# Keeping the split feed-forward weights in DRAM between the two token halves

## The chip, the cores and the metric

The kernel runs on one core of one Trainium2 chip. The metric is device time in microseconds for one execution of the whole layer; before the change the median of three runs is 2856.76 us (2854.7 to 2862.01).

## What is computed

One layer of a hybrid encoder on 2048 tokens of width 1024, float32 in and out. The attention part (differential attention in 4 heads, stick-breaking attention in 8) comes first and is not touched. The change lies in the last two lines, the SwiGLU feed-forward part with inner width 2816:

```
u   = rms_norm(h, norm1_w)
p   = u @ w_in                      # q, k, v of both attentions
h   = h + concat(y_diff, y_sb) @ w_out
u2  = rms_norm(h, norm2_w)
h   = h + (silu(u2 @ w_gate) * (u2 @ w_up)) @ w_down
```

## The kernel before

**Precision.** TensorE gets float16 operands, but the products are to be nearly float32. Each float32 operand is split in two float16 tiles, a rounded part `hi` and the remainder `lo`, and three products (hi·hi, lo·hi, hi·lo) are summed in PSUM.

**Strassen form.** Each of the three feed-forward products is cut in 2 x 2 blocks and computed with seven block products instead of eight (`quad` for gate and up, `down` for the third). For that the weight tile must be turned into seven block operands: four sums and differences of blocks, made in place in float32, and a split of each of the seven. The result is one tile `w16` of 128 x 7 x 2 x 512 float16 per weight and group of 256 inner columns.

**Loops.** The tokens are worked in two halves of 1024, and the inner width in NFG = 11 groups (`fg`) of 256: 22 steps, the first 11 for half 0, the rest for half 1. A step runs gate (84 matmuls), up (84) and, when two steps have been gathered, the down pass for both of them (168 matmuls) between its gate and its up. So a pair of steps is one without and one with a down pass. Residual rows are kept in DRAM (`hd`) and loaded (`hs`), added to and stored again in each down pass. The tokens' operands (`X`, seven tiles) stay in SBUF for a whole half; those of half 1 are still being built (`build_x`, with DMA transposes) while the first steps of half 0 run.

**A weight's way**, in `load_ffn`, for each of gate, up and down in every step: a stage tile `fst` (float32, 1 MB, two buffers for all three weights) is loaded. In half 0 its scale is found: ScalarE squares it into `sq` (one buffer), TensorE sums or transposes that (`fsc`), VectorE takes the maximum and makes the power-of-two scale. These scales are kept for half 1. Then, in both halves, four combinations on GpSimd (L99, three in place in `fst` and one into `sx`) and, four times, a rounding to `hi` (L210, ScalarE; now and then GpSimd) and a remainder `lo` on VectorE (L215). So each weight is loaded and split twice, once in each half, with the same result. The tiles of gate and up share two buffers (`wgu`), those of down have two (`wd`).

**Order.** Every engine runs its instructions in the order in which the program's scheduler, which has its own timeline of the program, puts them. Nearly all DMAs are issued by SP, one after the other: a DMA whose wait is not over holds up all behind it.

Of the kernel before, what the change touches and what calls it, by code (L numbers as in the profile page):

```python
# [21 lines left out]
S, D, P = 2048, 1024, 128  # L22
NT, KT, NC = S // P, D // P, S // 512
FF = 2816
NFG = FF // 256
# [14 lines left out]
XO = (10, 13, 14, 15, 11, 12, 15)  # L40
WO = (10, 14, 15)
CU = 3
WE = ("AP", "AP")
LE, SE, AE = "DP", "D", "P"


# [14 lines left out]
def block(tc, a, out):  # L61
    nc = tc.nc
    PE, ACT, DVE, POOL, SP = nc.tensor, nc.scalar, nc.vector, nc.gpsimd, nc.sync
    top = ExitStack()
    with top:
# [8 lines left out]
        def note(e, ns):  # L74
            load[e] += ns * KW[e]
# [98 lines left out]
        def across(dst, pt, cols):  # L174
            k = len(cols)
            for j, c in enumerate(cols):
                PE.matmul(pt[:, P * j : P * j + P], lhsT=c.to_broadcast([P, P]), rhs=id32[:], start=True, stop=True)
            DVE.tensor_reduce(dst, pt[:, : P * k], op=ALU.max, axis=AX.X)

        def scale_begin(pieces, junk=None):  # L180
            m0 = sm.tile([P, 4], F32, tag="m0", name=nm("m0"))
            for j, pc in enumerate(pieces):
                if junk is not None:
                    ACT.activation(junk, pc, AF.Square, accum_out=m0[:, j : j + 1])
                    note("A", 0.84 * int(np.prod(pc.shape[1:])) + 200)
                else:
                    DVE.tensor_reduce(m0[:, j : j + 1], pc, op=ALU.max, axis=AX.XY if len(pc.shape) > 2 else AX.X, apply_absolute_value=True)
                    note("D", 1.05 * int(np.prod(pc.shape[1:])) + 100)
            return [m0[:, j : j + 1] for j in range(len(pieces))]

        def scale_end(top_of, rW, pW, squares, sW):
            m1 = sm.tile([P, 1], F32, tag="m1", name=nm("m1"))
            top_of(m1[:])
            if squares:
                DVE.tensor_scalar(m1[:], m1[:], 1.0e-36, None, op0=ALU.max)
                exponents(m1[:], rW, pW)
            else:
                pow2(m1[:], rW, pW)
            DVE.tensor_scalar(sW[:], rW, 2.0 ** 10, None, op0=ALU.mult)
# [51 lines left out]
        with ExitStack() as ph1:  # L251
# [533 lines left out]
            op = out_proj()  # L785
# [13 lines left out]
        with ExitStack() as ph2:  # L799
# [14 lines left out]
            def stage(fg, nme, half):  # L814
                st = fw.tile([P, 2048], F32, tag="fst", bufs=2, name=nm("fst"))
                f0 = 256 * fg
                if nme == "d":
                    d = SP.dma_start(st[:].rearrange("p (f n) -> p f n", f=2), a["w_down"][0, f0 : f0 + 256, :].rearrange("(f p) n -> p f n", p=P))
                else:
                    d = SP.dma_start(st[:].rearrange("p (k n) -> p k n", k=KT), a["w_gate" if nme == "g" else "w_up"][0, :, f0 : f0 + 256].rearrange("(k p) n -> p k n", p=P))  # L820
                if half == 0 and fg == 0:
                    after_mt(d, WO["gud".index(nme)])
                return st

# [5 lines left out]
                    pass  # L830

            def load_ffn(half, fg, names, W):
                eng = "ADP" if half == 0 and fg == 0 else WE[half]
                sc = scales.setdefault(fg, {})
                for nme in names:
                    st = stage(fg, nme, half)
                    if half == 0:
                        r, p, sW = c1(), c1(), c1()
                        sq = fw.tile([P, 2048], BF16, tag="sq", bufs=1, name=nm("sq"))
                        if nme == "d":  # L840
                            cols = scale_begin([st[:]], sq[:])
                        else:
                            ACT.activation(sq[:], st[:], AF.Square)
                            note("A", 1900)
                    yield
                    late = nme == "d" and half == 1 and fg == NFG - 1
                    w16 = fw.tile([P, 7, 2, 512], F16, tag="wd" if nme == "d" and not late else "wgu", bufs=2, name=nm("w" + nme))
                    if half == 0:
                        pt = ps2.tile([P, 512], F32, tag="b", bufs=8, name=nm("fsc"))

                        def columns(m):
                            for k in range(KT):
                                PE.matmul(pt[:, :256], lhsT=ones[:], rhs=sq[:, 256 * k : 256 * k + 256], start=k == 0, stop=k == KT - 1)
                            DVE.tensor_reduce(m, pt[:, :256], op=ALU.max, axis=AX.X)

                        scale_end((lambda m: across(m, pt, cols)) if nme == "d" else columns, r[:], p[:], True, sW)
                        sc[nme] = (r, p, sW)
                    sW = sc[nme][2]
                    tte = "DP" if half == 0 and fg == 0 else "P"
                    sx = fw.tile([P, 512], F32, tag="sx", bufs=1, name=nm("sx"))  # L860

                    def put(o, src, n):
                        split_weight(w16[:, o : o + n, 0], w16[:, o : o + n, 1], src, 512 * n, sW, eng)

                    if nme == "d":
                        sv = st[:].rearrange("p (f h n) -> p h f n", f=2, h=2)
                        b11, b21, b12, b22 = sv[:, 0, 0], sv[:, 0, 1], sv[:, 1, 0], sv[:, 1, 1]
                        put(0, sv[:, 0], 2)
                        tt(sx[:], b22, b12, ALU.subtract, 512, tte)
                        tt(b12, b12, b11, ALU.subtract, 512, tte)  # L870
                        tt(b11, b22, b12, ALU.subtract, 512, tte)
                        tt(b21, b21, b11, ALU.subtract, 512, tte)
                        put(2, sv[:, 1], 2)
                        put(4, sv[:, 0], 2)
                        put(6, sx[:].unsqueeze(1), 1)
                    else:
                        sv = st[:].rearrange("p (d k f n) -> p d k f n", d=2, k=4, f=2)
                        xv = sx[:].rearrange("p (k n) -> p k n", k=4)
                        wv = w16[:].rearrange("p o s (k n) -> p o s k n", k=4)

                        def putk(o, src, n):
                            split_weight(wv[:, o : o + n, 0], wv[:, o : o + n, 1], src, 512 * n, sW, eng)

# [203 lines left out]
            W = {}  # L1087
# [86 lines left out]
```

## Time and profile before

| | |
|---|---|
| median of three runs | 2856.76 us |
| the profiled execution | 2849.59 us |
| its span, first to last instruction | 2847.8 us |
| mean granted TensorE clock | 0.957 |
| HBM read / written | 239.32 MB / 90.96 MB |
| `fst` loads | 66 of 1024 KB |

The feed-forward part begins at about 1480 us of the span; half 0 lasts to about 2150 and half 1 from there to the end. In the rows of groups, a line such as L99 or L215 is that of a helper that several weights use, so it is read with the tile's name. Times are from the span's start.

### The profile page before, as it was taken

Reading aid. Unit: us, or ns where it says so; the run is one execution under the profiler, and the core shown is the slowest. Engines: PE = TensorE matmul, PEld = TensorE weight load, DVE = VectorE, ACT = ScalarE, POOL = GpSimd, SP = SyncE. Lnnn points to the kernel's source line nnn. Section 1 sums busy time; section 2 is a strip of 40 time slices with the busy share of each in tenths; the row PEclk is TensorE's granted clock in tenths of the full one; section 3 lists DMA queues with packets and bytes.
Section 4 is the critical chain, followed back from the end, with each engine's and each line's share of the span. In section 5 each row is a group of like instructions: output and inputs, shape, how many; then the busy total and the mean of one; then the engine's idle time right before and its main releaser. Section 6 shows DMA issues by size and latency. Waiting matters only on the chain.

```text
span 2847.8 us, 45790 instructions
## 1 busy us (share of the span) xinstructions
PE 2519.3 (88%) x17052; PEld 1409.9 (50%) x17052; DVE 2229.5 (78%) x3922; ACT 1481.5 (52%) x2666; POOL 1703.5 (60%) x1133
## 2 busy tenths in 40 slices
PE   7998898888888777788888999899998999999997
PEld 4565556555555444477763444444443444444443
DVE  6898879787989999787638776877778868678675
ACT  4665656567787888656515443534433324334231
POOL 3577767664545545455627655656666667576663
PEclk9999999999999888999989999999999999999998
DMA  7778887889999898978876434242336442442424
GB/s 235 191 160 177 169 176 168 172 166 219 215 193 197 161 182 162 204 168 226 213 255 181 144 107 163 73 149 97 125 133 238 132 163 84 151 165 74 148 74 177
DMA packets 680094, 469.07 MB, mean 165 GB/s; under 512 B 520688, under 2 KB 610800, under 8 KB 678080
## 3 DMA queue, kind: packets, MB, share of 16 engines
q1 hardware_dynamic: 678048, 464.08, 63.1%
q8 instruction: 133, 2.18, 0.3%
q0 software_dynamic: 512, 1.36, 0.2%
q10 hardware_dynamic: 1312, 0.72, 0.1%
q14 instruction: 89, 0.73, 0.1%
HBM read 239.32 MB, written 90.96 MB: 116 GB/s over the span
## 4 chain that ended last, share of the span: by engine, by line
PE 21%; DVE 16%; DMA 7%; POOL 6%; issue 5%; ACT 3%; SPq 1%; DVEq 0%; POOLq 0%; ACTq 0%
PE pd L1008 11%; DVE wu L215 3%; PE pd L911 3%; POOL fst L99 3%; PE pm L911 3%; PE pa L911 3%; DVE wd L215 2%; DVE cg L99 2%; DMA fst<-in_w_down_dram 2%; DVE cg L976 1%; PE po L757 1%; DVE z L558 1%; DMA aT<-s 1%; DMA xcd<-b 1%; DMA b<-b 1%
## 5 line engine op out<-in xcount | busy, mean ns | idle before, releaser
L99 POOL TENSOR_TENSOR s<-z,s 128x1024 f16<-128x1024 f32 (+7 forms) x288 | 474.5, 1656 | 327.8 <-ACT s L90 299.5
L321 PE MATMUL pj<-w,xt 128*128 128x384 f16 x3072 | 576.2, 336 | 25.7 <-DVE st L331 9.6
L99 POOL TENSOR_TENSOR fst<-fst 128x512 f32<-128x512 f32 x193 | 348.3, 1805 | 225.2 <-DVE wg L215 98.0
L1008 PE MATMUL pd<-wd,act 128*128 128x512 f16 x1848 | 416.2, 384 | 30.0 <-DVE hs L1017 11.2
L321 PEld LDWEIGHTS <-xt 128*128 128x128 f16 x3072 | 301.4, 100 | 238.2 <-issue 45.0
L558 DVE TENSOR_TENSOR_SCAN z<-z,sc 128x512 f32<-128x512 f32 (+3 forms) x320 | 355.6, 1113 | 74.8 <-ACT sc L556 70.6
L449 PE MATMUL sc<-kT,qT 128*128 128x512 f16 (+3 forms) x1280 | 347.2, 362 | 72.7 <-DVE z L559 26.3
L459 PE MATMUL yp<-v,aT 128*128 128x64 f16 (+1 forms) x4896 | 281.3, 207 | 77.1 <-DMA aT<-s 76.2
L459 PEld LDWEIGHTS <-aT 128*128 128x128 f16 x4896 | 244.8, 101 | 168.6 <-DMA aT<-s 105.4
L911 PEld LDWEIGHTS <-wg 128*128 128x128 f16 x1848 | 185.8, 101 | 279.3 <-issue 76.2
L1008 PEld LDWEIGHTS <-act 128*128 128x128 f16 x1848 | 181.4, 99 | 256.6 <-issue 25.0
L911 PEld LDWEIGHTS <-wu 128*128 128x128 f16 x1848 | 182.1, 99 | 231.7 <-issue 19.2
L99 POOL TENSOR_TENSOR hs<-hs,cu 128x512 f32<-128x512 f32 x138 | 190.6, 1391 | 165.4 <-DVE cu L1017 66.4
L90 ACT CAST s<-z 128x384 f16<-128x384 f32 (+7 forms) x216 | 170.4, 790 | 139.2 <-DMA aT<-s 59.0
L1017 DVE SCALAR_TENSOR_TENSOR hs<-pd,c,hs 128x512 f32<-128x512 f32 x192 | 139.0, 745 | 131.0 <-PE pd L1008 98.6
L99 POOL TENSOR_TENSOR act<-cg,act 128x512 f16<-128x512 f32 x108 | 173.2, 1609 | 103.1 <-ACT act L970 103.1
L555 ACT ACTIVATE z<-sc,c 128x512 f32<-128x512 f32 (+3 forms) x320 | 203.8, 637 | 20.4 <-PE sc L449 10.5
L559 DVE TENSOR_TENSOR z<-sc,z 128x512 f32<-128x512 f32 (+3 forms) x320 | 193.3, 606 | 7.7
L556 ACT ACTIVATE sc<-sc,c 128x512 f32<-128x512 f32 (+3 forms) x320 | 196.0, 613 | 0.0
L757 PE MATMUL po<-wo,mt 128*128 128x256 f16 x1536 | 184.2, 279 | 13.0 <-DVE xf L760 12.5
L970 ACT CAST act<-cg 128x512 f16<-128x512 f32 x132 | 80.5, 615 | 212.1 <-DVE cg L976 124.8
L911 PE MATMUL pm<-X,wg 128*128 128x512 f16 x792 | 178.6, 379 | 1.0 <-POOL wg L214 1.0
(228 smaller groups left out, 4480.8 us busy)
## 6 DMA issues: line engine op xcount, KB each, us to landing
xt<-xs SPq DMA_DIRECT2D x112, 512.0 KB, 4.2
hs<-hd SPq DMA_DIRECT2D x96, 512.0 KB, 4.3
hd<-hs SPq DMA_DIRECT2D x80, 512.0 KB, 5.1
fst<-in_w_gate_dram SPq DMA_DIRECT2D x22, 1024.0 KB, 5.1
fst<-in_w_up_dram SPq DMA_DIRECT2D x22, 1024.0 KB, 5.3
fst<-in_w_down_dram SPq DMA_DIRECT2D x22, 1024.0 KB, 4.8
X<-xcd SPq DMA_DIRECT2D x14, 1024.0 KB, 9.6
wst<-in_w_in_dram SPq DMA_DIRECT2D x24, 512.0 KB, 6.5
```

What stands on the lines that cost most here:

```text
L90: ACT.copy(dst, src)
L99: (DVE if e == "D" else POOL).tensor_tensor(dst, a_, b_, op)
L321: PE.matmul(pj[:, :384], lhsT=xv[:, xi, kt, :], rhs=G["w"][:, wi, kt, :], start=n == 0, stop=n == 23)
L449: PE.matmul(sc[:, : 128 * w].rearrange("p (t n) -> p t n", n=P), lhsT=G["q"][i // 4][:, 2 - 2 * o + m, i % 4, :], rhs=G["k"][q][:, m, 0:w, ...
L459: PE.matmul(yp[:, y0 : y0 + wd], lhsT=aT[:, a_, :], rhs=v[:, v_ : v_ + wd], start=start and j == 0 and q == 0, stop=stop and j == nb - 1 a ...
L555: ACT.activation(om[:, lo:hi], sc[:, :w], AF.Sigmoid, scale=G["nkz"][:])
L556: ACT.activation(sc[:, :w], sc[:, :w], AF.Sigmoid, scale=G["kz"][:])
L558: DVE.tensor_tensor_scan(ov, ov, sc[:, :w], om[:, hi : hi + 1], op0=ALU.mult, op1=ALU.bypass)
L559: DVE.tensor_tensor(be[:, lo:hi], sc[:, :w], om[:, lo + 1 : hi + 1], ALU.mult)
L757: PE.matmul(po[:, sl], lhsT=mt[:, kt, P * xi : P * xi + P], rhs=wos[2 * h + n][wi][:, kt, :], start=q == 0, stop=q == 23)
L911: PE.matmul(ps_[:].rearrange("p (t n) -> p t n", n=P), lhsT=wv[:, wo, wi, 128 * kt : 128 * kt + 128], rhs=X[xo][:, :, xi, kt, :], start=st ...
L1008: PE.matmul(po[:], lhsT=act[:, ao, xi, 128 * j : 128 * j + 128], rhs=W["d"][:, wo, wi, :], start=start and u == 0 and q == 0, stop=u == nu ...
```

## The change

In half 0 the finished `w16` is also written to a DRAM tensor `split` (33 tiles of 1792 KB). In half 1 no stage tile is loaded and nothing is combined or split: the tile is read back from `split`, straight into its buffer. The engines that a split may use in half 0 stay the same (`WE[0]` and now `WE` are both ScalarE and GpSimd).

```diff
+        split = dr.tile([NFG, 3, P, 7 * 2 * 512], F16, name="split")
...
             def load_ffn(half, fg, names, W):
-                eng = "ADP" if half == 0 and fg == 0 else WE[half]
+                eng = "ADP" if fg == 0 else WE
                 sc = scales.setdefault(fg, {})
                 for nme in names:
-                    st = stage(fg, nme, half)
-                    if half == 0:
-                        r, p, sW = c1(), c1(), c1()
...
+                    if half == 1:
+                        yield
+                        late = nme == "d" and fg == NFG - 1
+                        w16 = fw.tile([P, 7, 2, 512], F16, tag="wd" if nme == "d" and not late else "wgu", bufs=2, name=nm("w" + nme))
+                        SP.dma_start(w16[:].rearrange("p o s n -> p (o s n)"), split[fg, "gud".index(nme)])
+                        W[nme] = w16
+                        continue
+                    st = stage(fg, nme)
+                    r, p, sW = c1(), c1(), c1()
...
                     W[nme] = w16
+                    SP.dma_start(split[fg, "gud".index(nme)], w16[:].rearrange("p o s n -> p (o s n)"))
```

Up to the feed-forward part the order of all engines is the same as before. Behind it the scheduler lays the work anew. Three places:

SP's queue in half 0, before, from the load of one step's gate weight on (`fst` is the stage tile, `hd` and `hs` the residual rows):

```order
L820 DMA fst_23158<-in_w_gate_dram 128x8x256
L818 DMA fst_23244<-in_w_down_dram 128x2x1024
L820 DMA fst_23339<-in_w_up_dram 128x8x256
L820 DMA fst_23500<-in_w_gate_dram 128x8x256
L818 DMA fst_23716<-in_w_down_dram 128x2x1024
L1055 DMA hd<-hs_23439 128x1024
```

and the same place now:

```order
L821 DMA fst_23182<-in_w_gate_dram 128x8x256
L899 DMA split<-wu_23093 128x7168
L819 DMA fst_23269<-in_w_down_dram 128x2x1024
L899 DMA split<-wg_23234 128x7168
L821 DMA fst_23365<-in_w_up_dram 128x8x256
L899 DMA split<-wd_23337 128x7168
L821 DMA fst_23527<-in_w_gate_dram 128x8x256
L899 DMA split<-wu_23434 128x7168
L819 DMA fst_23744<-in_w_down_dram 128x2x1024
L1061 DMA hd<-hs_23466 128x1024
```

Ahead of each stage load stands the write of the tile that was split from the same stage buffer before.

TensorE in the same step, a step of half 0 without a down pass, around the sum for the up tile's maximum (`fsc` from `sq`; `pm`, `pd`, `pa` are block products), before:

```order
L911 MATMUL pm_23364<-X_19838,wu_23070 128x512
L853 LDWEIGHTS ones
L853 MATMUL fsc_23409<-sq_23344,ones 128x256
...
L911 LDWEIGHTS wg_23210
L911 MATMUL pa_23442<-X_19828,wg_23210 128x512
...
L911 MATMUL pd_23346<-X_19840,wu_23070 128x512
```

and now:

```order
L917 MATMUL pm_23390<-X_19840,wu_23093 128x512
...
L917 MATMUL pd_23372<-X_19842,wu_23093 128x512
L858 LDWEIGHTS ones
L858 MATMUL fsc_23435<-sq_23370,ones 128x256
...
L917 MATMUL pa_23469<-X_19830,wg_23234 128x512
```

Here, and in one other of the four steady steps of half 0 without a down pass, the up tile's maximum has moved behind one more product of 12 matmuls (`pd`); in the two others it keeps its place.

VectorE in half 1, in a gate that is followed by a down pass, before (`cg` are gate blocks, `cu` up blocks, `wu` the next weight):

```order
L215 SCALAR_TENSOR_TENSOR wu_27260<-fst_27196,c_22407,wu_27260 128x2x512
L99 TENSOR_TENSOR cu_27247<-cg_27057,cg_27014 128x512
L215 SCALAR_TENSOR_TENSOR wu_27260<-fst_27196,c_22407,wu_27260 128x2x512
L927 TENSOR_TENSOR cg_27291<-pm_27293,cg_27291 128x512
L215 SCALAR_TENSOR_TENSOR wu_27260<-sx_27261,c_22407,wu_27260 128x512
L99 TENSOR_TENSOR cg_27014<-cg_27014,cg_27074 128x512
L99 TENSOR_TENSOR cg_27057<-cg_27014,cg_27057 128x512
L931 TENSOR_TENSOR cg_27320<-pm_27307,cg_27291 128x512
L99 TENSOR_TENSOR cg_27043<-cg_27043,cg_27057 128x512
L215 SCALAR_TENSOR_TENSOR wu_27260<-fst_27196,c_22407,wu_27260 128x2x512
L941 TENSOR_TENSOR cg_27351<-pd_27338,cg_27320 128x512
```

and now:

```order
L99 TENSOR_TENSOR cu_27735<-cg_27575,cg_27532 128x512
L99 TENSOR_TENSOR cg_27532<-cg_27532,cg_27590 128x512
L933 TENSOR_TENSOR cg_27767<-pm_27769,cg_27767 128x512
L99 TENSOR_TENSOR cg_27575<-cg_27532,cg_27575 128x512
L99 TENSOR_TENSOR cg_27561<-cg_27561,cg_27575 128x512
L937 TENSOR_TENSOR cg_27796<-pm_27783,cg_27767 128x512
L947 TENSOR_TENSOR cg_27825<-pd_27812,cg_27796 128x512
```

The four remainders of the split (L215) are gone from ahead of the eviction of `pd` (L941 before, L947 now), for whose buffer TensorE's next product waits. In half 1 SP's queue holds two reads for down weights at the end of each down pass and, behind them, up, gate, up, gate, each waiting for TensorE's last matmul on its buffer.

More of the change, by code (lines that the diff above doesn't have):

```diff
@@ L42 @@
 CU = 3
-WE = ("AP", "AP")
+WE = "AP"
 LE, SE, AE = "DP", "D", "P"
@@ L812, in after_mt, with stage @@
                 tc.add_manual_dep(d.ins, mts[k].ins.name, mybir.DependencyInfo(mybir.DependencyClass.NoSync, mybir.DependencyReason.DATA), reason="issue order")
-            def stage(fg, nme, half):
+            def stage(fg, nme):
                 st = fw.tile([P, 2048], F32, tag="fst", bufs=2, name=nm("fst"))
@@ L820, in stage @@
                     d = SP.dma_start(st[:].rearrange("p (k n) -> p k n", k=KT), a["w_gate" if nme == "g" else "w_up"][0, :, f0 : f0 + 256].rearrange("(k p) n -> p k n", p=P))
-                if half == 0 and fg == 0:
+                if fg == 0:
                     after_mt(d, WO["gud".index(nme)])
@@ L832, in load_ffn @@
             def load_ffn(half, fg, names, W):
-                eng = "ADP" if half == 0 and fg == 0 else WE[half]
+                eng = "ADP" if fg == 0 else WE
                 sc = scales.setdefault(fg, {})
                 for nme in names:
-                    st = stage(fg, nme, half)
-                    if half == 0:
-                        r, p, sW = c1(), c1(), c1()
[L839 to L844, printed above, removed]
-                    yield
[L846 to L857, printed above, removed]
@@ new lines, in load_ffn @@
+                    sq = fw.tile([P, 2048], BF16, tag="sq", bufs=1, name=nm("sq"))
+                    if nme == "d":
+                        cols = scale_begin([st[:]], sq[:])
+                    else:
+                        ACT.activation(sq[:], st[:], AF.Square)
+                        note("A", 1900)
+                    yield
+                    w16 = fw.tile([P, 7, 2, 512], F16, tag="wd" if nme == "d" else "wgu", bufs=2, name=nm("w" + nme))
+                    pt = ps2.tile([P, 512], F32, tag="b", bufs=8, name=nm("fsc"))
@@ L858, in load_ffn, with columns @@
+                    def columns(m):
+                        for k in range(KT):
+                            PE.matmul(pt[:, :256], lhsT=ones[:], rhs=sq[:, 256 * k : 256 * k + 256], start=k == 0, stop=k == KT - 1)
+                        DVE.tensor_reduce(m, pt[:, :256], op=ALU.max, axis=AX.X)
+                    scale_end((lambda m: across(m, pt, cols)) if nme == "d" else columns, r[:], p[:], True, sW)
+                    sc[nme] = (r, p, sW)
                     sW = sc[nme][2]
-                    tte = "DP" if half == 0 and fg == 0 else "P"
+                    tte = "DP" if fg == 0 else "P"
```

## The prediction

> **What bounds the kernel now.** I read the page's busy shares first, then busy time by stretch, the order in time of TensorE, VectorE and the DMA queue inside the feed-forward part, and the landings of the transfers.
>
> ```profile
> PE 2519.3 (88%) x17052; PEld 1409.9 (50%) x17052; DVE 2229.5 (78%) x3922; ACT 1481.5 (52%) x2666; POOL 1703.5 (60%) x1133
> ...
> 1480.00:1600.00 120.00, 104.70 (x450) 46.82 (x450) 104.35 (x152) 66.19 (x79) 81.16 (x49) 0.90 0.60 174
> 1600.00:2150.00 550.00, 515.62 (x2413) 238.64 (x2412) 406.72 (x577) 225.69 (x268) 332.35 (x212) 0.98 0.38 129
> 2200.00:2800.00 600.00, 572.27 (x2589) 255.18 (x2588) 443.45 (x441) 207.23 (x269) 392.05 (x244) 0.98 0.39 131
> ```
>
> The last three rows are the start of the first token half, the rest of it, and the second half; their columns are the stretch, then busy us and count of TensorE, weight loads, VectorE, ScalarE and GpSimd, granted clock, DMA share, GB/s. TensorE bounds both halves. How far it is from its own pace is told by the order of its work:
>
> ```profile
> 1868.23 18.29 PE L1008 MATMUL pd<-wd,act 128*128 128x512 f16 x84
> 1886.36 2.54 PE L911 MATMUL pa<-X,wu 128*128 128x512 f16 x11
> ...
> 2169.39 0.81 PE L1008 MATMUL pd<-wd,act 128*128 128x512 f16 x3
> ...
> 2201.85 3.75 PE L911 MATMUL pa<-X,wu 128*128 128x512 f16 x12
> ...
> 2318.33 2.54 PE L911 MATMUL pa<-X,wu 128*128 128x512 f16 x11
> ...
> 2742.14 2.72 PE L1008 MATMUL pd<-wd,act 128*128 128x512 f16 x11
> 2749.73 4.44 PE L911 MATMUL pd<-X,wg 128*128 128x512 f16 x12 [4.87 <-DVE cg L941]
> 2754.00 32.75 PE L1008 MATMUL pd<-wd,act 128*128 128x512 f16 x151
> 2786.59 2.54 PE L911 MATMUL pa<-X,wu 128*128 128x512 f16 x11
> ...
> 2806.66 0.81 PE L1008 MATMUL pd<-wd,act 128*128 128x512 f16 x3
> ```
>
> 84 matmuls take 1886.36 - 1868.23 = 18.13 us, 215.8 ns each. From 2201.85 (step 11's up) to 2806.66 (end of step 21's up) TensorE has 31 times 84 matmuls, 562.0 us at that pace, and takes 604.8: 42.8 us are lost. Four pairs of steps (2318.33 to 2786.59) take 117.1 us each for 108.8 of matmuls. The largest single loss is the wait for a VectorE eviction (L941) before the last gate product. Why VectorE is late there:
>
> ```profile
> 2733.30 1.56 DVE L215 SCALAR_TENSOR_TENSOR wu<-fst,c,wu 128x1024 f16<-128x1024 f32 x1 [0.65 <-ACT wu L210]
> 2736.34 2.28 DVE L215 SCALAR_TENSOR_TENSOR wu<-fst,c,wu 128x1024 f16<-128x1024 f32 x1
> 2745.04 2.28 DVE L215 SCALAR_TENSOR_TENSOR wu<-fst,c,wu 128x1024 f16<-128x1024 f32 x1
> 2748.98 0.69 DVE L941 TENSOR_TENSOR cg<-pd,cg 128x512 f32<-128x512 f32 x1
> ```
>
> VectorE has no idle of note between 2733 and 2749; the splits stand ahead of the eviction in its queue.
>
> **The second half: what goes.** Per weight tile three in-place GpSimd combinations and one into sx, four ScalarE roundings and four VectorE remainders go, for 33 tiles:
>
> ```profile
> L99 POOL TENSOR_TENSOR fst<-fst 128x512 f32<-128x512 f32 x184 | 333.2, 1811 | 190.0 <-DVE wg L215 95.7 <-DVE wd L215 47.3 <-DVE wu L215 41.0
> L215 DVE SCALAR_TENSOR_TENSOR wd<-fst,c,wd 128x1024 f16<-128x1024 f32 x63 | 100.8, 1607 | 30.2 <-ACT wd L210 30.2
> L210 ACT ACTIVATE wd<-fst,c 128x1024 f16<-128x1024 f32 x63 | 70.7, 1145 | 131.8 <-POOL fst L99 60.5 <-PE pd L1008 40.5 <-DVE c L199 16.9
> ```
>
> That frees about 33 x 4 x 1.6 = 211 us of VectorE, 33 x 4 x 1.8 = 238 of GpSimd and 33 x 4 x 1.1 = 145 of ScalarE, all beside TensorE; on the path count only the 42.8 us. VectorE falls from 443 to about 232 of 600 us, so the waits for L941 should go; I leave 1 us for each of five step pairs and take **-38** (ends -28, if a third stays, and -43). What would be late next there is the weight read.
>
> Each tile read is 7 x 2 x 512 x 2 bytes x 128 = 1.835 MB for 1.049 MB before. It is issued when the buffer's last matmul has run and is wanted, in the steps without a down pass, 61 matmuls = 13.2 us later (the sequence of products). A landing:
>
> ```profile
> X<-xcd SPq DMA_DIRECT2D x14, 1024.0 KB, 9.6
> ...
> DMA to landing us min/median/max: 4.7/5.1/14.0
> ...
> 1441.00:1449.00 8.00, 5.31 (x49) 4.61 (x48) 0.48 (x1) 0.00 (x0) 0.00 (x0) 1.00 0.98 383
> 2138.00:2150.00 12.00, 12.00 (x59) 5.63 (x57) 5.13 (x14) 3.22 (x4) 1.16 (x1) 1.00 0.98 359
> ```
>
> (median for X, queued behind one another; then the f32 stage tile; then stretches in which the rings were full, 383 and 359 GB/s.) 4.7 us for the first megabyte and 0.79 MB / 383 = 2.1 give 6.8 us: **0** (upper end: 1.75 x 9.6 = 16.8 us, 3.6 late, twice a pair, +36). I take the lower, as the DMA share here is 0.39.
>
> **The first half: what comes.** 33 writes of 1.835 MB, each issued right ahead of the stage load that takes over the buffer; the write waits for the same last remainder on VectorE as that load, so the wait itself adds nothing and SP pays 0.4 us of issue. But the load's bytes stand behind the write's: 1.835 / 383 = **4.8 us** (5.1 at 359). That transfers queue so is seen once:
>
> ```profile
> 1435.45 2.71 SPq L1097 DMA_DIRECT2D X<-xcd  x3
> ...
> 1440.50 0.38 SPq L820 DMA_DIRECT2D fst<-in_w_gate_dram  x1
> ...
> 1453.08 1.91 ACT L843 ACTIVATE sq<-fst 128x2048 bf16<-128x2048 f32 x1 [20.67 <-DMA fst<-in_w_gate_dram]
> ```
>
> A 1 MB load behind three X tiles was ready 12.6 us after its issue, for 4.7 unhindered. The HBM page of the Trainium skill (HBM Reference, Specifications) has a core that streams alone at about 425 GB/s; by that the write would hold the rings 4.3 us and the costs below would fall by about a tenth. No row here has stores alone, so I keep 383.
>
> Where is a load not covered? TensorE's maximum over a tile (fsc) needs the square (sq) of the landed tile:
>
> ```profile
> 1697.33 0.37 SPq L820 DMA_DIRECT2D fst<-in_w_up_dram  x1
> 1702.38 1.91 ACT L843 ACTIVATE sq<-fst 128x2048 bf16<-128x2048 f32 x1
> 1704.78 1.04 PE L853 MATMUL fsc<-sq,ones 128*128 128x256 bf16 x8
> ...
> 1911.36 0.38 SPq L820 DMA_DIRECT2D fst<-in_w_gate_dram  x1
> 1922.42 1.04 PE L853 MATMUL fsc<-sq,ones 128*128 128x256 bf16 x8
> ...
> 1940.74 0.37 SPq L820 DMA_DIRECT2D fst<-in_w_up_dram  x1
> 1945.84 1.91 ACT L843 ACTIVATE sq<-fst 128x2048 bf16<-128x2048 f32 x1 [0.56 <-DMA fst<-in_w_up_dram]
> 1947.80 1.86 PE L853 MATMUL fsc<-sq,ones 128*128 128x256 bf16 x8 [2.74 <-ACT sq L843]
> ```
>
> In steps without a down pass the up tile has no slack: at 1704.78 it is just in time, at 1947.80 TensorE already waits. The gate tile there has 1922.42 - 1911.36 = 11.1 us from issue to use; load 5.1, write 4.8 and square 1.9 make 11.8, about 0.9 late with the issue. So the up maximum comes 4.8 + 0.9, less 0.4 of slack, = 5.3 us later where its place stays (two of the four such steps), and 5.7 - 2.6 = 3.1 where the scheduler puts it 12 matmuls (2.6 us) later (the other two). In the steps with a down pass the maximum stands some 20 us after the load: 0, covered by the down matmuls. A stall of 5 us also slows what follows: the 12 matmuls after the wait of 4.87 took 4.44 us where 12 x 215.8 ns is 2.6, some 1.8 us. Sum 2 x (5.3 + 1.8) + 2 x 3.1 = **+20** (ends 0, if the new places hide it all, and 35).
>
> The Trainium skill (TensorE: Matmul & The Clock Gate, Part 1: The HAM clock gate) says that an idle window of about 3.4 us halves the clock until as long a busy one has passed. It agrees with the 1.8 and speaks against the change: only stalls past that length would pay it, so with all four under it the 20 would be 17.
>
> At the start (1480 to 1600) six loads in a row are tight, in two chains of three, one per stage buffer, among build_x's transposes:
>
> ```profile
> 1572.38 0.80 PE L177 MATMUL fsc<-id,m 128*128 128x128 f32 x2 [2.02 <-ACT sq L184]
> 1584.23 1.03 PE L853 MATMUL fsc<-sq,ones 128*128 128x256 bf16 x8 [1.17 <-ACT sq L843]
> ```
>
> All three late by 4.8 would be 14; the new order puts several loads ahead of transposes they stood behind, which may hide all. I take half, **+7** (0 to 15). In the five down passes a write falls among the chains of hd stores and hs loads; TensorE's wait on that chain is small:
>
> ```profile
> 2127.51 6.85 PE L1008 MATMUL pd<-wd,act 128*128 128x512 f16 x31 [0.69 <-DVE hs L1017]
> ```
>
> I take **+3** (0 to 5 x 4.8 = 24, near the low end).
>
> Between the halves, 2169.39 to 2201.85, TensorE runs 96 matmuls (20.7 us) in 32.5, held by evictions behind splits. Those of step 11 go, but two reads and a write (5.5 MB, 14.4 us at 383 GB/s) join rings that are 0.98 full; the product that needs the last X tile now comes after most of the down pass. **-3** (-12 to +14).
>
> Removed combinations in the first half: none. Sum: -38 + 20 + 7 + 3 - 3 = **-11 us**. The profiled execution took 2849.6 us (span 2847.8), 7.2 under the median of 2856.8; carried over, 2845.8.
>
> **Rivals.** *The gain is eaten* (no change): start at 15, down passes at 8, the rest as above: +2 us, or down to -6 with half of that, about 2855. For it: six tight loads with no slack; against: the moved checks. *Writes hidden* (faster still): the 30 us of costs shrink to 8, -33, 2824; for it speaks a DMA share of 0.38; against, that loads are issued in the very moment the write is. *The writes hold the rings longer* (slower): every further us costs about 4 in the four steps and 2.3 at the start; the sum is zero at 4.8 + 11 / 6.3 = 6.5 us and past the 0.3% bound (8.6 us, about what this measurement can tell from no change) at 7.9. At 8.5 us it is +12, 2869. For it: X's 9.6 us a megabyte; against: both full stretches. *Reads late in the second half* (slower): landing 16.8, net -11 + 36 = +25, 2882; it decides from 13.2 us on; against: one read at a time, share 0.39.
>
> **Chances.** Forecast (-9 to -28) 0.37, writes hidden 0.13: faster 0.50. Gain eaten 0.30: the same. Longer writes 0.13, late reads 0.07: slower 0.20. The likeliest case alone spans 2828 to 2848; the range, with a bit cut off both the hidden and the late ends, 2822 to 2870.
>
> **What would show it.** Right: second half pairs of steps near 110 us, no wait for L941 there; first half waits of TensorE for sq of 4 to 6 us in steps without down, stage loads landing at 9 to 10 us. Wrong: stage loads that land at 5 us (hidden), TensorE weight loads that wait for DMA wu or wg (late reads), or first half pairs longer by more than 10 us.

## The result and the profile after

The changed kernel takes 2827.2 us (median of six runs, 2820.2 to 2830.8) beside 2857.5 for the kernel before (six runs, 2851.8 to 2870.9): ratio 0.9879, 95% interval 0.9862 to 0.9896. That is 30 us faster, where 11 were forecast. The profiled execution took 2822.4 us (span 2820.6; before 2847.8), so the traces have 27.2 us between them. Lines of the changed code stand 1 to 7 higher: L941 is now L947, L843 is L850, L853 is L858, L970 is L976.

The page's busy times, to be read beside those of before:

```profile
PE 2505.3 (89%) x17052; PEld 1410.6 (50%) x17052; DVE 2003.0 (71%) x3780; ACT 1358.3 (48%) x2534; POOL 1452.7 (52%) x1011
```

VectorE lost 226.5 us, GpSimd 250.8 and ScalarE 123.2, near the forecast 211, 238 and 145. The next two views are busy time by stretch, of before and of after. The cuts are TensorE's first matmuls of gate(0), gate(2), up(2), up(10) and up(11), and the end of up(21); the number is the step. So the rows are the start, the first down pass, four steady pairs of steps, the passage between the halves, and the second half. Columns as in the prediction.

```profile
1482.83:1585.10 102.27, 88.13 (x374) 38.91 (x373) 87.83 (x126) 55.33 (x66) 70.31 (x43) 0.90 0.65 182
1585.10:1639.79 54.69, 54.12 (x256) 24.88 (x254) 44.55 (x61) 21.62 (x27) 38.02 (x26) 1.00 0.42 146
1639.79:2134.20 494.41, 460.60 (x2153) 213.14 (x2152) 368.73 (x519) 208.94 (x247) 301.47 (x191) 0.98 0.35 120
2134.20:2201.85 67.65, 58.91 (x255) 25.52 (x254) 56.41 (x63) 25.11 (x32) 43.69 (x27) 0.94 0.65 234
2201.85:2806.66 604.81, 577.08 (x2614) 257.54 (x2613) 444.48 (x444) 209.06 (x272) 393.26 (x245) 0.98 0.39 130
```

```profile
1486.14:1598.33 112.19, 85.71 (x374) 39.03 (x373) 100.70 (x130) 55.75 (x65) 77.37 (x45) 0.88 0.83 258
1598.33:1660.12 61.79, 57.74 (x255) 25.34 (x254) 38.43 (x55) 20.95 (x27) 33.21 (x24) 0.93 0.58 201
1660.12:2162.71 502.59, 467.20 (x2154) 215.65 (x2153) 365.70 (x517) 205.27 (x243) 290.71 (x188) 0.97 0.59 206
2162.71:2217.32 54.61, 54.61 (x256) 24.96 (x254) 36.21 (x52) 14.74 (x21) 22.39 (x16) 1.00 0.91 358
2217.32:2781.29 563.97, 563.97 (x2614) 255.68 (x2613) 236.54 (x316) 99.32 (x155) 170.92 (x135) 1.00 0.51 180
```

The second column, the length, is the reading. Start +9.9, first down pass +7.1, steady pairs +8.2, passage -13.0, second half -40.8; with +3.3 ahead of gate(0) and -1.9 behind up(21) that is -27.2. In the last two rows TensorE is busy for the whole stretch: nothing holds it from up(10) to the end of up(21).

TensorE's waits in the four steady pairs, of before and then of after (total us, times, longest):

```profile
PE pd L911 <- DVE cg L941: 19.8, 8, 4.5
PE fsc L853 <- ACT sq L843: 5.6, 2, 2.9
PE fsc L177 <- ACT sq L184: 3.6, 2, 2.2
PE pd L911 <- DVE cu L941: 2.9, 2, 1.5
```

```profile
PE fsc L858 <- ACT sq L850: 28.1, 8, 6.7
PE fsc L178 <- ACT sq L185: 5.4, 2, 3.7
PE pd L917 <- DVE cg L947: 1.7, 2, 0.9
```

Waits for a square grew from 9.2 to 33.5 us, where 17 more were forecast (2 x 5.3 + 2 x 3.1); waits for VectorE's evictions fell from 22.7 to 1.7, which was not forecast. All in all TensorE is hardly more idle in the four pairs: length less busy time is 33.8 us before and 35.4 after. The rest of the +8.2 is busy time, 460.6 to 467.2 us for the same matmuls, at a granted clock of 0.97 for 0.98: the waits have become fewer and longer, and long ones are followed by a slow stretch (see the account of the prediction below).

The landings in the changed kernel, and the place in the first down pass where TensorE waits for ScalarE and ScalarE for build_x's stores:

```profile
split<-wg SPq DMA_DIRECT2D x11, 1792.0 KB, 6.9
wd<-split SPq DMA_DIRECT2D x11, 1792.0 KB, 8.3
fst<-in_w_gate_dram SPq DMA_DIRECT2D x11, 1024.0 KB, 9.4
fst<-in_w_up_dram SPq DMA_DIRECT2D x11, 1024.0 KB, 10.1
fst<-in_w_down_dram SPq DMA_DIRECT2D x11, 1024.0 KB, 8.9
xcd<-b SPq DMA_DIRECT2D x6, 512.0 KB, 10.2
...
1620.62 1.66 ACT L976 CAST act<-cg 128x512 f16<-128x512 f32 x3 [11.14 <-DMA xcd<-b]
1621.29 10.93 PE L1014 MATMUL pd<-wd,act 128*128 128x512 f16 x36 [3.95 <-ACT act L976]
```

Stage loads land at 9 to 10 us as forecast (about 5 before). build_x's stores (xcd<-b) land at 10.2; before, the same six took 4.5:

```profile
xcd<-b SPq DMA_DIRECT2D x6, 512.0 KB, 4.5
```

They read a buffer (b16) that takes a place of the act tiles, so up(1)'s first rounding waits for the last of them, and the first down pass for the rounding.

### The profile page after: what moved, and what is told of

Its sections match the earlier page's. It is cut to its first block, busy times and chain, and to the rows that moved or that the text cites. A ratio compares the mean times of both kernels' runs of the same rounds, so it can differ in the third digit from the quotient of the medians.

```text
span 2820.6 us, 45459 instructions
## 1 busy us (share of the span) xinstructions
PE 2505.3 (89%) x17052; PEld 1410.6 (50%) x17052; DVE 2003.0 (71%) x3780; ACT 1358.3 (48%) x2534; POOL 1452.7 (52%) x1011
## 4 chain that ended last, share of the span: by engine, by line
PE 36%; DVE 11%; DMA 9%; issue 5%; POOL 4%; ACT 4%; SPq 1%; DVEq 0%; POOLq 0%; ACTq 0%
PE pd L1014 14%; PE pm L917 8%; PE pa L917 6%; PE pd L917 5%; DVE z L559 4%; DMA aT<-s 2%; POOL s L99 2%; DVE wd L216 1%; DMA fst<-in_w_up_dram 1%; DMA fst<-in_w_down_dram 1%; PE po L758 1%; DVE z L560 1%; PE pj L322 1%; DMA xcd<-b 1%; DMA b<-b 1%
## 5 line engine op out<-in xcount | busy, mean ns | idle before, releaser
L99 POOL TENSOR_TENSOR act<-cg,act 128x512 f16<-128x512 f32 x118 | 165.3, 1410 | 284.7 <-ACT act L976 284.7
L99 POOL TENSOR_TENSOR hs<-hs,cu 128x512 f32<-128x512 f32 x138 | 178.5, 1301 | 249.4 <-DVE cu L1023 103.3
L917 PEld LDWEIGHTS <-wg 128*128 128x128 f16 x1848 | 184.9, 100 | 243.6 <-issue 33.8
L1014 PEld LDWEIGHTS <-act 128*128 128x128 f16 x1848 | 181.7, 98 | 239.2 <-issue 14.6
L99 POOL TENSOR_TENSOR fst<-fst 128x512 f32<-128x512 f32 x94 | 173.0, 1840 | 122.2 <-DVE wg L216 37.6
L976 ACT CAST act<-cg 128x512 f16<-128x512 f32 x132 | 80.4, 616 | 235.3 <-DVE cg L982 187.9
```

The lines of the kernel that those rows point to most:

```text
L99: (DVE if e == "D" else POOL).tensor_tensor(dst, a_, b_, op)
L917: PE.matmul(ps_[:].rearrange("p (t n) -> p t n", n=P), lhsT=wv[:, wo, wi, 128 * kt : 128 * kt + 128], rhs=X[xo][:, :, xi, kt, :], start=st ...
L1014: PE.matmul(po[:], lhsT=act[:, ao, xi, 128 * j : 128 * j + 128], rhs=W["d"][:, wo, wi, :], start=start and u == 0 and q == 0, stop=u == nu ...
```

## The experiments

Each run is read by the same cuts (us; the last stage here ends where up(21) begins):

| run | gate(0)-gate(2) | -up(2) | -up(10) | -up(11) | -up(21) | median |
|---|---|---|---|---|---|---|
| before | 102.3 | 54.7 | 494.4 | 67.7 | 584.7 | 2857.5 |
| after | 112.2 | 61.8 | 502.6 | 54.6 | 543.9 | 2827.2 |
| writes only | 111.3 | 61.8 | 507.5 | 63.5 | 588.6 | 2880.3 |
| reads only | 102.5 | 56.3 | 491.4 | 55.3 | 543.3 | 2800.2 |
| load first | 103.1 | 72.5 | 493.3 | 54.6 | 543.9 | 2817.3 |
| step 11 splits | 111.9 | 61.6 | 507.5 | 62.8 | 544.2 | 2837.9 |
| same order, small writes | 109.6 | 57.7 | 490.4 | 54.6 | 543.9 | 2808.1 |
| writes from ScalarE | 121.8 | 54.6 | 521.8 | 58.9 | 543.9 | 2853.1 |
| six writes from ScalarE | 114.1 | 57.5 | 492.2 | 54.6 | 543.9 | 2819.3 |
| written twice | 119.1 | 87.1 | 527.6 | 54.9 | 543.9 | 2881.6 |
| second step not written | 106.7 | 56.1 | 492.2 | 55.6 | 544.9 | 2810.5 |
| second and third not | 106.8 | 56.0 | 492.2 | 54.9 | 551.5 | 2813.3 |

The part ahead of gate(0), which the change does not touch, ends between 1482.8 and 1499.0 us in these profiles, so stages tell more than totals. They repeat well: from up(2) to up(8) after, writes only and step 11 splits take 377.6, 377.6 and 377.7 us. The stages are those of one profiled execution, which for writes only and for small writes is 8 us above the median of the last column, for six writes from ScalarE 11 below it. The kernel before took 2859 to 2860 us beside the experiments; ratios are against those runs.

**Writes only.**

```diff
+                    if half == 0:
+                        SP.dma_start(split[fg, "gud".index(nme)], w16[:].rearrange("p o s n -> p (o s n)"))
```

on the kernel before, whose second half stays.

> The 33 tiles are written in the first token half, but the second half loads and splits the original weights again as in the kernel before. Theory (the stage terms add): the first half costs what it costs in the changed kernel, 28 us (1482.83 to 2134.20 is 651.4 us before, 1486.14 to 2162.71 is 676.6 after, and 3 more ahead of it), nothing is earned behind it, and the stretch between the halves is not shorter than the 67.7 us of before: about 2857.5 + 28 = 2885 us, stage loads landing at 9 to 10 us. Rival (the gain between the halves belongs to the new order of the first half's last steps, which the writes bring, and not to the splits of step 11 that are gone): that stretch is near 55 us here too, and the time is about 2872.

Ratio 1.0070 (1.0052 to 1.0088): the writes alone cost 20 us by the medians. By stages the first half, gate(0) to up(10), goes from 651.4 to 680.7: +29, in an execution 8 us above its median beside one of the kernel before 8 below. The passage is 63.5, which is neither 67.7 nor 55; but the pair ahead of it takes 129.9 for 126.5, and from up(8) to up(11) both together take 193.4 us for 194.1 before and 179.6 in the changed kernel. The writes earn nothing there: the first theory holds, with a stage's end moved.

**Reads only.**

```diff
-                    SP.dma_start(split[fg, "gud".index(nme)], ...)
+                    if fg == 0:
+                        SP.dma_start(split[fg, "gud".index(nme)], ...)
...
-                        SP.dma_start(w16[:]..., split[fg, "gud".index(nme)])
+                        SP.dma_start(w16[:]..., split[0, "gud".index(nme)])
```

> Only the three tiles of the first feed-forward step are written; every step of the second half reads those three instead of its own, so the output leaves out the other ten steps' right weights in the second token half. Theory (the terms add): the first half is near that of before (no write from the second step on, stage loads at about 5 us), the second half earns 41 us and the stretch between the halves 13: about 2857.5 - 54 + 3 = 2806 us. Rival (the new waits for late loads only stand where VectorE waits stood, so that leaving the writes out brings those back): the waits for VectorE's evictions L941/L947 sum to 20 us or more in the first half, its four pairs from up(2) to up(10) stay at 494 us as before, and the time still falls by the start and the first down pass alone: about 2827 - 17 = 2810. What tells them apart is therefore the four pairs: under the first both the VectorE waits and the waits for sq are gone (about 480 us), under the second the pairs are 494 with the VectorE waits back.

Ratio 0.9787 (0.9768 to 0.9805), some 60 us faster than before: the second half and the passage earn theirs without the writes, and three writes in the first step cost next to nothing (158.8 us to up(2) for 157.0). The pairs take 491.4 us with 20.7 us of waits for VectorE, so the rival held: without late loads those waits are back. Most of them are on one line:

```profile
PE pd L918 <- DVE cg L948: 18.5, 8, 4.5
```

The order is another here too, so this run alone does not say which of the two brought them back.

**Load first.** The write of a tile is issued right behind the load that takes over its stage buffer:

```diff
                     st = stage(fg, nme)
+                    flush(1)
...
-                    SP.dma_start(split[fg, "gud".index(nme)], w16[:]...)
+                    pending.append((fg, nme, w16))
```

where flush(n) issues the oldest pending writes until n are left.

> All 33 tiles are written and read as in the changed kernel, but each write is issued right behind the stage load that takes over the buffer, not ahead of it. Theory (what costs in the first half is that the load's bytes stand behind the write's): stage loads land at 5 to 6 us again, TensorE's waits for sq are gone, and the first half comes down from 677 us to near 651: about 2827 - 22 = 2805 us. Rival (the write's bytes hold the rings, whichever goes first, and put off the next chain of hd and hs transfers or the next load): landings of 7 us or more, first half above 665, 2816 or more.

Ratio 0.9848 (0.9831 to 0.9865). Loads land at 6.5, 6.5 and 6.4 us, the pairs are back at 493.3 and the start at 103.1, but the first down pass takes 72.5 us for 61.8, which is more than the start won:

```profile
fst<-in_w_up_dram SPq DMA_DIRECT2D x11, 1024.0 KB, 6.5
xcd<-b SPq DMA_DIRECT2D x6, 512.0 KB, 10.8
...
1625.97 1.66 ACT L985 CAST act<-cg 128x512 f16<-128x512 f32 x3 [20.10 <-DMA xcd<-b]
1626.64 9.24 PE L1023 MATMUL pd<-wd,act 128*128 128x512 f16 x30 [15.00 <-ACT act L985]
```

Of the 22 us expected 10 came. The theory is right for the loads and wrong for the first down pass, where it is not the loads but build_x's stores, still behind the writes in SyncE's one queue, that TensorE ends up waiting for. That is what the rival had in mind, a write that puts off other transfers, though with another chain; its first half above 665 us (668.8) and its 2816 or more came, its landings of 7 us or more did not.

**Step 11 splits.**

```diff
-                    if half == 1:
+                    if half == 1 and fg > 0:
```

with the load and split of before for step 11.

> As the changed kernel, but the first step of the second token half (step 11) loads and splits its three weights as before; the other ten steps read. Theory (the 13 us between the halves come from the 12 remainders of step 11 that VectorE no longer has there): the stretch from step 10's up to step 11's up goes back to about 67 us, the time to about 2827 + 13 = 2840. Rival (they come from the new order, or from reads that are there earlier than splits could be, whatever VectorE does): the stretch stays under 60, the time under 2832.

Ratio 0.9922 (0.9903 to 0.9941), 11 us slower than the change. The passage takes 62.8 and the last steady pair 129.8, in the changed kernel 54.6 and 124.95: 8.2 + 4.9 = 13.1, nearly all of the 14.6 us that the change won over the two stretches together (194.1 before, 179.6 in the changed kernel). This stretch, beside the fourth row of after:

```profile
2168.72:2231.54 62.82, 56.85 (x256) 25.07 (x254) 50.52 (x60) 22.20 (x29) 36.95 (x23) 0.98 0.77 298
```

VectorE works 50.5 us of it, for 36.2 without those splits. The theory held on the size, with the place spread over two stretches.

**Same order, small writes.** The program is scheduled as the changed kernel; then 30 of its writes are cut to 64 columns, so that every engine's order stays and only the bytes go:

```diff
+    def small(i):
+        if isinstance(i, mybir.InstDMACopy) and i.outs[0].memref.startswith("split") and i.outs[0].offset >= 3 * P * 7168:
+            return i.__replace__(ins=cut(i.ins[0]), outs=cut(i.outs[0]))   # cut: ap [[7168, 128], [1, 64]]
+        return i
```

> The changed kernel with its own order kept instruction by instruction on every engine, but 30 of the 33 writes (all but those of the first step) move 64 of 7168 columns, 16 KB instead of 1792; the second half reads the first step's three tiles in every step, so the output leaves out the other steps' right weights there. It tells what took away the 21 us of VectorE waits that the first half's four pairs of steps (up(2) to up(10)) lost. Theory (overlap: the new waits for late loads stand where TensorE waited for VectorE before, so that VectorE catches up meanwhile): with the loads on time again the VectorE waits L947 come back, 15 us or more, and the pairs stay near 494 us as before. Rival (the scheduler's other order took them away): they stay under 6 us, the waits for sq fall to 10 or less, and the pairs take about 480. The whole time: about 2800 under the first, 2788 under the second.

Ratio 0.9818 (0.9796 to 0.9839), 19 us under the change. Neither theory is quite right, and the time is 8 us above the nearer of the two. Its landing of a stage load, and the waits of the four pairs:

```profile
fst<-in_w_gate_dram SPq DMA_DIRECT2D x11, 1024.0 KB, 5.4
...
PE fsc L858 <- ACT sq L850: 24.6, 8, 4.6
PE pd L917 <- DVE cg L947: 1.9, 2, 0.9
```

The waits for VectorE stay away (the rival), but most of those for the square stay too, with loads that land at 5.4 us; and the pairs take 490.4 us, 4 less than before. So in this order TensorE meets the square first and VectorE is ready by then. The reason, for the wait shown here, is on ScalarE; the load and its square of step 4's gate tile, in the changed kernel and then in this run:

```profile
1685.49 0.43 SPq L821 DMA_DIRECT2D fst<-in_w_gate_dram  x1
...
1697.26 0.69 ACT L965 ACTIVATE cg<-pa,c 128x512 f32<-128x512 f32 x1 [4.03 <-POOL act L99]
1697.85 1.90 ACT L850 ACTIVATE sq<-fst 128x2048 bf16<-128x2048 f32 x1
1699.80 1.87 PE L858 MATMUL fsc<-sq,ones 128*128 128x256 bf16 x8 [3.46 <-ACT sq L850]
1702.74 4.16 PE L917 MATMUL pd<-X,wg 128*128 128x512 f16 x12
```

```profile
1691.62 0.43 SPq L821 DMA_DIRECT2D fst<-in_w_gate_dram  x1
...
1703.40 0.69 ACT L965 ACTIVATE cg<-pa,c 128x512 f32<-128x512 f32 x1 [4.04 <-POOL act L99]
1703.99 1.90 ACT L850 ACTIVATE sq<-fst 128x2048 bf16<-128x2048 f32 x1
1705.94 1.86 PE L858 MATMUL fsc<-sq,ones 128*128 128x256 bf16 x8 [3.46 <-ACT sq L850]
```

The square starts 12.4 us after the load's issue in both, since the scheduler put it behind a SiLU (L965) that waits for GpSimd. The wait is 3.46 us with the bytes and without, and this pair takes 125.6 us in both runs; what the bytes cost lies in the three other pairs. The gate product behind it starts 42.6 us after up(2) (1702.74 - 1660.12). The same product in the kernel before, where up(2) began at 1639.79:

```profile
1681.99 4.23 PE L911 MATMUL pd<-X,wg 128*128 128x512 f16 x12 [3.81 <-DVE cg L941]
```

It started 42.2 us after up(2). One wait stands where the other stood. This match is shown for the first of the four pairs; the last has the same wait of 3.46 us in the same place. Elsewhere the places differ: in the changed kernel the long waits for an up tile's square end 68 to 70 us behind the up with which the pair begins, and the other waits for VectorE that went ended 62 to 63 and 86 to 89 us behind it. That VectorE catches up while TensorE waits for squares ahead of them is likely, and not shown.

From gate(0) to up(10) the kernel before takes 651.4 us, this run 657.7 and the changed kernel 676.6: the order, with the three whole writes of the first step, costs 6, the bytes of the other thirty 19. In the four pairs alone the order gains 4 and the bytes cost 12.2; up to up(2) the order costs 10 and the bytes 6.7.

**Writes from ScalarE.** Load first, with ACT.dma_start for the write:

```diff
-                    SP.dma_start(split[g, "gud".index(k)], w[:]...)
+                    ACT.dma_start(split[g, "gud".index(k)], w[:]...)
```

> All tiles are written and read; each write is issued from ScalarE's queue, behind the stage load that takes over the buffer. It tells whether the write costs by standing ahead in SyncE's queue, or by the rings that all transfers share. Theory (queue: hs, hd and build_x's transposes stand behind the write in SyncE's one queue, which is why xcd<-b landed in 10.2 us for 4.5 before and the first down pass began 18 us late in the run with the load first): here xcd<-b lands in 6 us or less, gate(2) to up(2) is back near 56 us and the time is about 2817 - 15 = 2802. Rival (the 16 engines are shared whichever queue issues): xcd<-b at 8 us or more, gate(2) to up(2) above 65, stage loads at 7 to 9 us since they now share with the write instead of going first, 2815 to 2830.

Ratio 0.9972 (0.9960 to 0.9984), 26 us slower than the change. It parts the two harms only in part. xcd<-b lands at 4.8 us and the first down pass takes 54.6, so what held build_x's stores was SyncE's queue. What that is worth in time is not shown, since the start grew to 121.8 and gate(0) to up(2) comes to 176.3 us, beside 175.5 with the load first. The loads land late again, and ScalarE waits for them:

```profile
fst<-in_w_up_dram SPq DMA_DIRECT2D x11, 1024.0 KB, 9.9
xcd<-b SPq DMA_DIRECT2D x6, 512.0 KB, 4.8
...
ACT sq L859 <- DMA fst<-in_w_up_dram: 68.6, 8, 12.6
```

A load and a write issued in the same moment by two queues get in each other's way, and the load (9.7 to 9.9 us) is as late as if it stood behind the write (8.9 to 10.1). The pairs take 130 us each, in yet another order, so the 26 us are not parted into order and landings. Neither forecast of the time held.

**Six writes from ScalarE.** `(ACT if g < 2 else SP).dma_start(...)` in the same place.

> As the run with the load first, but the six writes of the first two feed-forward steps, which fall among build_x's transposes, are issued from ScalarE's queue, the other 27 from SyncE's. Theory (queue): gate(2) to up(2) falls from 72 to about 56 us and the rest stays as in the run with the load first, about 2817 - 15 = 2802. Rival (shared engines): gate(2) to up(2) stays above 65, 2812 or more.

Ratio 0.9845 (0.9823 to 0.9867), no better than load first. The first down pass came down to 57.5 as the theory has it, but the start went up to 114.1: 171.6 us for both, beside 175.5. Most of the theory's gain was paid back next door.

**Written twice.**

```diff
+                    SP.dma_start(split2[fg, "gud".index(nme)], w16[:].rearrange("p o s n -> p (o s n)"))
```

behind the first write, split2 being a second place.

> The changed kernel with each of the 33 tiles written twice, to two places, one write behind the other ahead of the stage load. Theory (a write ahead costs a load its own time in the rings, and VectorE's waits that could hide it are used up): stage loads land near 9.5 + 4.8 = 14.3 us, the eight tight loads of the four pairs add 4.8 us each, 38 us, and the start and the first down pass some 17: about 2827 + 55 = 2882. Rival (half or more of a later landing is hidden, in VectorE's waits or in places that the scheduler moves): 2850 or less.

Ratio 1.0072 (1.0054 to 1.0090), 54 us over the change for 55 expected, but otherwise spread: pairs +25 for 38, start and first down pass +32 for 17. Loads land at 13.2 to 13.9 us. The second write costs the first half 57 us (733.8 for 676.6) where the first cost 25. The theory's reason, that no waits for VectorE are left to hide behind, did not hold: the pairs have 15.0 us of them again, in yet another order. Why the second write costs more than twice the first stays open.

**Second step not written.** Load first; the second step (fg 1) is not written and is split again in the second half:

```diff
-                    if half == 1:
+                    if half == 1 and fg not in (1,):
...
+                    if half == 0 and fg not in (1,):
+                        pending.append((fg, nme, w16, tiles[0]))
```

> Load first, as in the run of that name, but the three tiles of the second feed-forward step, which are split while build_x's transposes run, are not written; the second half loads and splits those three again and reads the other 30. Theory (the start pays because the writes of that step stand among build_x's chains): first gate to third up (gate(0) to up(2)) comes down from 175.6 us to about 159, as in the run that wrote only the first step's tiles, the step that splits again costs about 4 us in the second half (8.3 us a pair of steps before), and the time is about 2817 - 16 + 5 = 2806. Rival (the third step's two writes there do the same harm): that stretch stays above 168 and the time at 2814 or more.

Ratio 0.9823 (0.9804 to 0.9843): faster than the kernel before by 49 us and than the change by 17, with intervals that do not touch. Ten of the 17 are those of the load first; the 7 us beyond that run are within overlapping intervals, so the three writes are better read by stage. Its first, second and last stages:

```profile
1490.88:1597.60 106.72, 84.08 (x373) 38.23 (x372) 93.26 (x127) 55.46 (x65) 73.77 (x45) 0.93 0.79 240
1597.60:1653.68 56.08, 56.08 (x255) 25.34 (x254) 41.94 (x59) 21.06 (x27) 33.99 (x23) 0.96 0.57 184
2201.50:2746.42 544.92, 544.22 (x2522) 246.45 (x2520) 248.57 (x321) 105.28 (x160) 187.71 (x142) 1.00 0.49 175
```

The start and first down pass take 162.8 us (159 expected, 175.5 with those writes), so three writes held 13 us there; splitting one step again costs 1 us of the second half and 1 of the passage, not 5. VectorE is busy for 249 of 545 us in that half, so it has room for one step's splits.

**Second and third step not written.** `(1, 2)` for `(1,)`.

> As the run without the second step's writes, and without the third step's too; the second half splits two steps again and reads nine. Theory: gate(0) to up(2) is near 158 us here in any case, the second half pays about 9 us, so about 2817 - 17 + 9 = 2809. Rival (the third step's writes are what holds the start): the start falls here and not in the other, and this one is the faster of the two by 5 us or more.

Ratio 0.9836 (0.9817 to 0.9856). The start is the same to 0.1 us, so the third step's writes do no harm there, and the second half pays 7.6 us for two steps in a row. The theory held, with a time 4 us too low; the start came out 5 us above it and the second half 1.4 below.

## Why the prediction came out as it did

The direction and the range were right; the size was not: -27.2 us between the profiles for -11. Two terms failed by asking too much: the passage between the halves, where transfers were charged that nothing waits for, and the steady pairs, where new waits were added without taking off the old ones. That the time lies inside the range owes something to luck: the start and the first down pass came out 10 us above the sum, and without that error the time would lie below the range.

- **Second half, -38:** measured -40.8. Pairs take 108.8 us and there is no wait at all, so the 1 us kept per pair was too careful. **Reads, 0:** right. They land at 7.3 to 8.3 us (6.8 forecast, 13.2 allowed), and TensorE is never idle in that stretch. The late reads of the rival did not come.
- **Between the halves, -3 (-12 to +14), measured -13.0: the step that fell outside its own bounds.** The reasoning saw that the evictions wait behind splits there, and then gave most of it back because reads and a write would join full rings (the core's 16 DMA engines, whose busy share the views give). They did fill them (share 0.91, 358 GB/s in the stretch), and TensorE waited for nothing: none of those transfers is wanted at once. With the write or without it the stretch takes about 55 us (reads only 55.3, small writes 54.6); with the splits of step 11 the 13 us are gone.
- **Steady pairs and down passes, +20 and +3, measured +8.2: the largest error in us, -15.** The landing was right in kind and a little high in size: 4.0, 4.6 and 3.6 us later than in the same order without the bytes, where 4.8 was forecast. The HBM page of the Trainium skill (HBM Reference, Specifications) gave an estimate of 4.3 by its rate of 425 GB/s for a core that streams alone; the measured mean of 4.1 is nearer to that than to the 4.8 of the 383 GB/s taken. The waits for squares grew by 24.3 us for 16.8, mostly not for the landing, since 24.6 us of such waits stay when the bytes are gone. What failed is that new waits were added to the old ones: 21 us of waits for VectorE went, and with them idle time grew by 1.6 us in all. What did cost is the clock: 6.6 us more busy time, where the sum had 3.6 for two slow stretches. In the order of the changed kernel without the bytes the pairs take 490.4, so the bytes cost 12.2 and the order gave 4 back. A small slip besides: the gate tile's 0.9 us of lateness is 0.7 by its own terms (11.8 less 11.1), or 1.1 with the issue, which moves the sum by under 1 us.
- **Start, +7 (0 to 15), and the first down pass: measured +9.9 and +7.1.** The term counted late stage loads and not build_x's own stores, which stand in the same queue and hold a place of the act tiles: 4.0 of the down pass's 7.1 us are the wait for them. It also had the new order as a possible help, and with small writes that order takes 10 us more up to up(2), the three whole writes included. With the load first, leaving three writes out brought 13 us back. This was the one way in which the change was worse than forecast.
- **The first half as a whole** came to +25.2 (651.4 to 676.6) for a forecast of 30, because the errors of the pairs and of the start cancel in part. Set out against the sum: passage -10, pairs -15, start and first down pass +10, second half -3, and +1.4 ahead of and behind all that, which makes the 16 us.
- **The slow stretch after a stall, 1.8 us:** right for one stall, but counted for two only, where the changed kernel's pairs have seven waits of 3.46 us or more (three in the kernel before). The 12 matmuls of the gate product soon behind the wait of 3.46 took 4.16 us where 2.6 is their pace. In the changed kernel's steady pairs those seven are each followed by a loss of 1.7 to 2.9, by the spacing of the matmuls behind them, and the waits under 2 us by none. The Trainium skill (TensorE: Matmul & The Clock Gate, Part 1: The HAM clock gate) puts the limit at about 3.4 us of idle time. This trace agrees for the waits above it; in the kernel before a wait of 2.74 us already cost 1.7 and one of 2.85 nothing, so no sharp limit shows here.
- **Rivals.** "Writes hidden" (2824) is nearest in time and not what happened: the writes cost 25 us in the first half. "Longer writes" was decided by landings: a write delays a load by 4, not by the 6.5 us at which the gain would have been gone. Writing twice, with loads at 13 to 14 us, cost 57 us more. "The gain is eaten" had the start right (it and the first down pass took 17 us more) and was outweighed by the pairs and the passage. "Reads late" did not come, as said above.

What stays open: why the start takes 109.6 us with small writes, in the order of the changed kernel, against 102.3 before. The first step's three whole writes and the order are both in it. Reads only has the same three whole writes, in an order of its own, and takes 102.5, which points to the order; no run keeps the order and leaves those three out.

## What to carry to other kernels

Before a new wait is added to a sum, ask which wait stood at that place before: two waits that end at the same moment cost one, and only an order held fixed tells order from bytes. Read busy time beside waits: here idle time hardly grew in the steady pairs, and most of the cost was the slow clock behind longer waits. Ring share is no price by itself; ask of each transfer in a full stretch whether somebody wants it now. When writes are put on a queue, list every chain that uses the queue, and leave out the few writes that fall among a tight chain: here, with the load first, three of 33 writes cost 13 us of the start, and doing their work again cost 2.

## What the hardware showed that was not expected

- A 1 MB load behind a 1.835 MB store on one queue lands at 8.9 to 10.1 us (changed kernel); with the two issued at the same moment by two queues at 9.7 to 9.9 (writes from ScalarE); ahead of the store on one queue at 6.4 to 6.5 (load first); with the store cut to 16 KB at 5.3 to 5.5 (small writes). Here a second queue won the load nothing; being first did.
- The store itself lands at 6.7 to 6.9 us when it goes first and at 10.2 to 10.4 when the load does.
- TensorE ran 563.97 us of the second half without one gap that the profile shows, at a granted clock of 1.00, beside a DMA share of 0.51 and 180 GB/s.
